# The last eight rows of a diffusion layer: second halves finished one row later and stored from GpSimd, and the inverse root from two sums on GpSimd

## The chip, the cores and the metric

The program runs on one core of one Trainium2 chip. The time is device time of one execution in microseconds (us); three runs of the kernel before gave a median of 1449.69 us (1447.68 to 1451.36).

## The reference, cut to what matters

One layer over 1024 tokens of 1024 values: normalisation, a combined projection into retention and differential attention, an output projection with a gated residual, then normalisation, a gated MLP with a depthwise convolution and a second gated residual. The change touches only the last two lines, the residual of the MLP and the final RMSNorm:

```
x = x + g1 * y_lat
h2 = rms_norm(x, norm2_g[l]) * (1.0 + sc2) + sh2
x = x + g2 * conv_ffn(h2, w_up[l], conv_w[l], conv_b[l], w_down[l])
...
return rms_norm(x, final_g)
def rms_norm(x, g):
    xf = x.astype(jnp.float32)
    y = xf * lax.rsqrt(jnp.mean(xf * xf, axis=-1, keepdims=True) + EPS)
    return (y * g.astype(jnp.float32)).astype(x.dtype)
```

## The kernel before, in words

The kernel computes float32 products from three passes on TensorE (`passes`, L127): each operand is split into a high and a low part, and high by high, high by low and low by high are added up in PSUM. ScalarE makes the high part (L908, L1227), VectorE the low part (L909, L1228).

The last stage (from L1211 on) is the down projection of the MLP, by a scheme of block sums and differences that needs seven block products in place of eight. The 1024 tokens are eight **rows** (tiles of 128 tokens), the 1024 output columns two **halves** of 512. `acc[t]` in SBUF is row t, 128 partitions by 1024. PSUM banks `c1` and `c2` hold four rows of one half each. When the products that fill the other three quarters of the output are done, they are copied or added into `acc` (L1265, L1270). What is left is the first half of rows 4 to 7, in `c1[0]` to `c1[3]`: eleven pairs of block operands, of which the first seven run over all four rows at once (L1333), each followed by `rows_before(m)` for m below 4, and the last four run row by row (L1337), so that `c1[0]` is complete first and `c1[3]` last.

A row is finished in these steps, and the names are used below:

- **load**: the row's residual `x1t` comes from DRAM on SyncE's DMA queue (L1274), into one of four buffers;
- **product** (L1276), VectorE: times the gate `g2bc`; for rows 4 to 7 the first half is read from PSUM;
- **sum** (L1277), VectorE: plus the residual;
- **square** (L1279), ScalarE: squares half a row and adds them up into one value per token, `sm4[:, t, c]`;
- **two small operations** on VectorE, 128x1 each: the two half sums are added (L1282), then divided by 1024 and EPS is added (L115, in `rsqrt`);
- **power**, GpSimd (L116): to the power of minus one half;
- **scale**, VectorE (L1287): times the power and times `fg`, the final gain. Rows 0 to 3 are scaled whole (128x1024) and stored from SyncE's queue (L1288). Rows 4 to 7 have had their second half multiplied by `fg` early (L1328, the **gain product**), so at the end ScalarE scales that half (L1343, the **second-half scale**) and VectorE the first (L1287), with one store each, both from SyncE's queue (L1344, L1288).

`rows_before(m)` does the second half of row m, finishes row m, and does the second half of row 4 + m. The code is written in this order, but a scheduler in the framework sets the final order of instructions on each engine from estimates of its own, and each engine then works through its own list strictly in that order; waits are on semaphores. An instruction that waits holds up all that stands behind it on its engine.

Of the kernel before, what the change touches and what calls it, by code (L numbers as in the profile page):

```python
# [11 lines left out]
AF = mybir.ActivationFunctionType  # L12
ALU = mybir.AluOpType
# [4 lines left out]
P = 128  # L18
D = 1024
# [10 lines left out]
EPS = 1e-6  # L30
# [43 lines left out]
def kernel(  # L74
# [16 lines left out]
    nc = tc.nc  # L91
# [17 lines left out]
    mhalf = kp.tile([P, 32], F32, name="mhalf")  # L109
# [4 lines left out]
    def rsqrt(out_ap, in_ap, mul, eps, n):  # L114
        nc.vector.tensor_scalar(out=out_ap, in0=in_ap, scalar1=mul, scalar2=eps, op0=ALU.mult, op1=ALU.add)  # L115
        nc.gpsimd.tensor_tensor(out=out_ap, in0=out_ap, in1=mhalf[:, :n], op=ALU.pow)  # L116
# [36 lines left out]
    with ExitStack() as p1:  # L153
# [495 lines left out]
        with tc.tile_pool(name="rc0", bufs=1) as r0:  # L649
# [20 lines left out]
            acc = r0.tile([P, 8], F32, name="acc")  # L670
# [58 lines left out]
        class Unit:  # L729
# [57 lines left out]
            def rstd(self):  # L787
                nc.vector.scalar_tensor_tensor(out=self.ss, in0=self.e, scalar=EPS * P, in1=self.ss, op0=ALU.mult, op1=ALU.add)
                self.pool_ins = nc.gpsimd.tensor_tensor(out=self.ss, in0=self.ss, in1=mhalf[:, :1], op=ALU.pow)
# [248 lines left out]
    def bank(name, pool=None):  # L1038
        return (next(bank_cycle) if pool is None else pool).tile([P, 512], F32, name=name, tag="bank")
# [49 lines left out]
    with ExitStack() as p4:  # L1089
# [93 lines left out]
        C = 512  # L1183
# [8 lines left out]
        def step(pd, a, b, first, last, more=False, ts=range(4)):  # L1192
            for t in ts:
                passes(pd[t], tuple(g[:, t * P : (t + 1) * P] for g in a), b, first, last, more)

        c1 = [bank(f"c1_{t}", psB if t < 2 else psC) for t in range(4)]
# [14 lines left out]
    with ExitStack() as p5:  # L1211
# [6 lines left out]
        def a_pair(i, m, n=2, alone=False):  # L1218

            raw = raw_load(next(slots), a_d[i][m].rearrange("p c (a b) -> p (c a) b", b=P)) if n == 2 else wst.tile([P, KD, P], F32, name=next(slots))  # L1220
            if n == 1:
                nc.sync.dma_start(out=raw[:, 0:4, :], in_=a_d[i][m][:, 0, :].rearrange("p (a b) -> p a b", b=P))
            raw = flat(raw)[:, : n * C]
            if alone:
                return [split1(raw[:, c * C : (c + 1) * C]) for c in range(n)]
            o = dop.tile([P, 2, 2 * C], F32R, name="ghl")
            nc.scalar.copy(o[:, 0, : n * C], raw)  # L1227
            nc.vector.tensor_tensor(out=o[:, 1, : n * C], in0=raw, in1=r32(o[:, 0, : n * C]), op=ALU.subtract)  # L1228
            return [tuple(o[:, a, c * C : (c + 1) * C] for a in range(2)) for c in range(n)]
# [25 lines left out]
        acc = [fin.tile([P, D], F32, name=f"acc{t}") for t in range(NT)]  # L1255
        g2bc = fin.tile([P, D], F32, name="g2bc")
        nc.sync.dma_start(out=g2bc, in_=g2_d)
        fg = fin.tile([P, D], F32, name="fg")
        nc.sync.dma_start(out=fg, in_=rows[0, R_FG : R_FG + D].partition_broadcast(P))
        sm4 = fin.tile([P, NT, 2], F32, name="sm4")  # L1260
        halves = [slice(0, C), slice(C, D)]

# [9 lines left out]
        def residual(t, c, src=None):  # L1272
            xt = fin.tile([P, C], F32, name="x1t", bufs=4)
            nc.sync.dma_start(out=xt, in_=x1_d[t][:, halves[c]])  # L1274
            dst = acc[t][:, halves[c]]
            nc.vector.tensor_tensor(out=dst, in0=dst if src is None else src, in1=g2bc[:, halves[c]], op=ALU.mult)  # L1276
            nc.vector.tensor_tensor(out=dst, in0=dst, in1=xt, op=ALU.add)  # L1277
            jk = fin.tile([P, C], BF16, name="jk", bufs=2)
            nc.scalar.activation(jk, dst, AF.Square, accum_out=sm4[:, t, c : c + 1])  # L1279

        def rstd(t):
            nc.vector.tensor_tensor(out=sm4[:, t, 0:1], in0=sm4[:, t, 0:1], in1=sm4[:, t, 1:2], op=ALU.add)  # L1282
            rsqrt(sm4[:, t, 0:1], sm4[:, t, 0:1], 1.0 / D, EPS, 1)

        def scaled(t, c0, c1_):
            x_ = acc[t][:, c0:c1_]
            nc.vector.scalar_tensor_tensor(out=x_, in0=x_, scalar=sm4[:, t, 0:1], in1=fg[:, c0:c1_], op0=ALU.mult, op1=ALU.mult)  # L1287
            nc.sync.dma_start(out=out[t * P : (t + 1) * P, c0:c1_], in_=x_)  # L1288
# [5 lines left out]
        for m in range(M):  # L1294
            s2, s1 = a_pair(1, m)
            t1 = split1(W[m, 0, 0])
            less(W[m, 0, 0], W[m, 1, 1], W[m, 0, 0])
            step(c1, s2, split1(W[m, 0, 0]), False, m == M - 1, True)
            step(c2, s1, t1, m == 0, m == M - 1)
            less(W[m, 1, 0], W[m, 1, 0], W[m, 0, 0])  # L1300
            if m < 4:
                first_difference(M - 4 + m)
            if 2 <= m < 6:
                residual(m - 2, 0)
# [16 lines left out]
        def rows_before(m):  # L1321
            if m < 4:
                residual(m, 1)
                rstd(m)
                scaled(m, 0, D)
                residual(4 + m, 1)
                dst = acc[4 + m][:, C:]
                nc.vector.tensor_tensor(out=dst, in0=dst, in1=fg[:, C:], op=ALU.mult)  # L1328
# [4 lines left out]
        for m in range(M - 4):  # L1333
            step(c1, a22s[m], T4s[m], False, False, True)
            rows_before(m)
        late_ops = list(zip(a22s, T4s))[M - 4 :]
        for t in range(4):  # L1337
            for i, ops in enumerate(late_ops):
                step(c1, *ops, False, i == 3, True, [t])
            r = 4 + t  # L1340
            residual(r, 0, c1[t])
            rstd(r)
            nc.scalar.activation(acc[r][:, C:], acc[r][:, C:], AF.Copy, scale=sm4[:, r, 0:1])  # L1343
            nc.sync.dma_start(out=out[r * P : (r + 1) * P, C:], in_=acc[r][:, C:])  # L1344
            scaled(r, 0, C)


def shape_constants():
# [75 lines left out]
```

## Time and profile before

| What | Value |
| --- | --- |
| Median of 3 runs | 1449.69 us (1447.68 to 1451.36) |
| Span of the profiled execution, first to last instruction | 1444.3 us |
| Between the span and the median | 5.4 us |
| Mean granted TensorE clock | 0.992 |
| TensorE busy | 1391.0 us (96%) |
| VectorE busy | 1013.2 us (70%) |
| ScalarE busy | 738.7 us (51%) |
| GpSimd busy | 336.4 us (23%) |

The profile gives the span of the profiled execution, from its first instruction to its last; what a timed run has beside that is not in the trace. Busy time of one engine overlaps that of the others. A timeline row gives the start and the duration in us, then engine, line, operation, output and inputs, shapes and count; in square brackets at its end stands how long the engine was idle before it and what released it. PE is TensorE, DVE VectorE, ACT ScalarE, POOL GpSimd, SPq the DMA queue of SyncE.

### The profile page before, as it was taken

The numbers are of one execution on the slowest core, as the hardware profiler recorded it, in microseconds if no ns is written. First come the engines' busy times: TensorE is split into PE (matmuls) and PEld (weight loads), VectorE is DVE, ScalarE is ACT, GpSimd is POOL, SyncE is SP. The second block draws the span as 40 slices with busy tenths as digits, with TensorE's granted clock in tenths as the row PEclk, the third lists the DMA queues.
The fourth block names the chain that finished last, engine by engine and source line by source line (L and its number), as shares of the span: only waits on it lengthen the run. The fifth ranks groups of instructions, "written<-read, shape, count | busy, mean of one in ns | idle before, by whom it ended". The sixth has DMA issues, their size and how long they took to land.

```text
span 1444.3 us, 19462 instructions
## 1 busy us (share of the span) xinstructions
PE 1391.0 (96%) x6924; PEld 1143.5 (79%) x6924; DVE 1013.2 (70%) x1509; ACT 738.7 (51%) x1409; POOL 336.4 (23%) x450
## 2 busy tenths in 40 slices
PE   7999999999899989999999999999999999999996
PEld 2587888788778779999888877888888888888885
DVE  4687454443677588889455988788777777998457
ACT  4565212232355688998414654555555545455533
POOL 0220000022688422431121043222223320000001
PEclk9999999999999999999999999999999999999999
DMA  7548754466456676680422122222222224952224
GB/s 283 218 144 292 241 190 161 161 190 189 129 160 194 161 180 157 149 150 2 187 77 85 73 89 110 110 109 99 86 90 106 109 109 166 391 208 103 102 95 175
DMA packets 107529, 217.77 MB, mean 151 GB/s; under 512 B 8932, under 2 KB 47332, under 8 KB 106536
## 3 DMA queue, kind: packets, MB, share of 16 engines
q1 hardware_dynamic: 99304, 191.62, 38.2%
q0 software_dynamic: 8128, 24.91, 7.8%
q8 instruction: 55, 0.90, 0.3%
q14 instruction: 42, 0.34, 0.1%
HBM read 159.08 MB, written 57.41 MB: 150 GB/s over the span
## 4 chain that ended last, share of the span: by engine, by line
PE 69%; DVE 8%; issue 6%; DMA 6%; POOL 3%; ACT 3%; SPq 0%; POOLq 0%; DVEq 0%; ACTq 0%
PE pv L774 5%; PE pA L742 5%; PE chain L130 5%; PE chain L132 5%; PE chain L131 5%; PE c L132 4%; PE c L131 4%; PE c L130 4%; PE pn L132 3%; PE pn L130 3%; PE pn L131 3%; PE third L132 2%; PE third L130 2%; PE third L131 2%; PE pt L762 2%
## 5 line engine op out<-in xcount | busy, mean ns | idle before, releaser
L130 PE MATMUL chain<-T,whi 128*128 128x512 f32 x264 | 103.7, 393 | 5.8 <-ACT ub L1152 3.1
L130 PE MATMUL pl<-hT,whi 128*128 128x512 f32 x256 | 107.6, 422 | 0.7 <-ACT hT L583 0.7
L131 PE MATMUL chain<-T,whi 128*128 128x512 f32 x264 | 103.5, 392 | 0.0
L132 PE MATMUL chain<-T,wlo 128*128 128x512 f32 x264 | 103.1, 391 | 0.0
L131 PE MATMUL pl<-hT,whi 128*128 128x512 f32 x256 | 101.6, 397 | 1.6 <-DVE sm L115 1.3
L132 PE MATMUL pl<-hT,wlo 128*128 128x512 f32 x256 | 100.9, 394 | 0.0
L745 DVE TENSOR_REDUCE mt<-pA 128x1 f32<-128x1280 f32 x64 | 95.3, 1490 | 3.3 <-PE pA L742 1.2
L742 PE MATMUL pA<-ks,qhl 128*128 128x512 f32 (+1 forms) x384 | 91.4, 374 | 5.0 <-ACT p L749 5.0
L132 PE MATMUL c<-whi,ghl 128*128 128x512 f32 x232 | 90.4, 390 | 0.2 <-DVE ghl L1228 0.2
L130 PE MATMUL c<-whi,ghl 128*128 128x512 f32 x232 | 90.3, 389 | 0.0
L131 PE MATMUL c<-wlo,ghl 128*128 128x512 f32 x232 | 90.2, 389 | 0.0
L749 ACT ACTIVATE p<-pA,mt 128x1280 f32<-128x1280 f32 x64 | 85.5, 1336 | 4.6 <-DVE mt L745 4.5
L116 POOL TENSOR_TENSOR sm<-sm,mhalf 128x1 f32<-128x1 f32 x26 | 16.7, 641 | 294.9 <-DVE sm L115 294.8
L1057 POOL TENSOR_TENSOR cmb<-wrb 128x512 f32<-128x512 f32 x20 | 26.8, 1341 | 250.1 <-DMA wrb<-w_up 135.9
L908 ACT CAST whi<-cmb 128x512 fp32r<-128x512 f32 x62 | 38.6, 623 | 87.1 <-PE chain L131 65.3
L742 PEld LDWEIGHTS pA<-ks,qhl 128*128 128x128 f32 x384 | 68.8, 192 | 17.6 <-ACT p L749 6.1
L130 PE MATMUL pn<-whi,hT 128*128 128x512 f32 x192 | 77.8, 405 | 0.0
L774 PE MATMUL pv<-va,aT 128*128 128x128 f32 x640 | 77.0, 275 | 0.1
L399 ACT ACTIVATE st<-pn 128x512 f32<-128x512 f32 x30 | 17.9, 598 | 114.7 <-PE pn L132 97.2
L908 ACT CAST whi<-wra 128x512 fp32r<-128x512 f32 x55 | 33.7, 622 | 82.9 <-PE third L131 42.3
L132 PE MATMUL pn<-whi,hT 128*128 128x512 f32 x192 | 75.5, 393 | 0.0
L131 PE MATMUL pn<-wlo,hT 128*128 128x512 f32 x192 | 75.1, 391 | 0.0
(320 smaller groups left out, 4006.2 us busy)
## 6 DMA issues: line engine op xcount, KB each, us to landing
wm<-w_mod SPq DMA_DIRECT2D x32, 512.0 KB, 4.4
raw<-w_in SPq DMA_DIRECT2D x28, 512.0 KB, 4.5
wra<-w_up SPq DMA_DIRECT2D x24, 512.0 KB, 3.2
wrb<-w_up SPq DMA_DIRECT2D x23, 512.0 KB, 3.5
W<-w_down SPq DMA_DIRECT2D x44, 256.0 KB, 6.0
ad<-s SPq DMA_DIRECT2D x20, 512.0 KB, 3.7
wra<-ad SPq DMA_DIRECT2D x20, 512.0 KB, 3.2
wrb<-ad SPq DMA_DIRECT2D x18, 512.0 KB, 4.1
```

The source lines that it names most:

```text
L116: nc.gpsimd.tensor_tensor(out=out_ap, in0=out_ap, in1=mhalf[:, :n], op=ALU.pow)
L130: mm(ps, lh, rh, start=first, stop=False, skip_group_check=more)
L131: mm(ps, lh, rl, start=False, stop=False, skip_group_check=more)
L132: mm(ps, ll, rh, start=False, stop=last, skip_group_check=more)
L399: nc.scalar.activation(st.rearrange("p h e -> p (h e)"), pt, func, scale=scale)
L742: mm(self.pa[m][:, c0:c1], self.q[:, i, m, qs], self.k[:, m, c0:c1], start=(i == 0), stop=(i == 1))
L745: nc.vector.tensor_reduce(out=self.mt[:, m : m + 1], in_=self.pa[m][:, :LK], axis=AX.X, op=ALU.min)
L749: nc.scalar.activation(self.p[m], self.pa[m][:, :LK], AF.Exp, scale=-1.0, bias=self.mt[:, m : m + 1], accum_out=self.s[:, m : m + 1])
L762: nc.tensor.transpose(self.pt[g][:, i, :], self.p[0][:, (4 * g + i) * P : (4 * g + i + 1) * P], ident)
L774: mm(self.pv, self.aT[:, c, :], self.v[:, c, :], start=(c == 0), stop=(c == NKT - 1))
L908: nc.scalar.copy(hi, src)
L1057: nc.gpsimd.tensor_tensor(out=s1, in0=b1, in1=b2, op=ALU.add)
```

## The change

Four edits, all in the last stage:

1. `fg` is multiplied by the square root of 1024 once, on GpSimd, right after it is loaded. With that the division of the sum by 1024 is no longer needed.
2. After the square of a second half, GpSimd adds 1024 times EPS to that half's sum (128x1).
3. `rstd` no longer uses VectorE: GpSimd adds the two sums (128x1) and takes the power.
4. For rows 4 to 7 the finishing steps (second-half scale, both stores, scale) move into `finished(r)`, which is called after the next row's product, sum, square and power; the store of the second half is issued from GpSimd's queue in place of SyncE's.

```
         fg = fin.tile([P, D], F32, name="fg")
         nc.sync.dma_start(out=fg, in_=rows[0, R_FG : R_FG + D].partition_broadcast(P))
+        nc.gpsimd.tensor_scalar(out=fg, in0=fg, scalar1=float(D) ** 0.5, scalar2=None, op0=ALU.mult)
...
             nc.scalar.activation(jk, dst, AF.Square, accum_out=sm4[:, t, c : c + 1])
+            if c:
+                nc.gpsimd.tensor_scalar(out=sm4[:, t, 1:2], in0=sm4[:, t, 1:2], scalar1=D * EPS, scalar2=None, op0=ALU.add)
 
         def rstd(t):
-            nc.vector.tensor_tensor(out=sm4[:, t, 0:1], in0=sm4[:, t, 0:1], in1=sm4[:, t, 1:2], op=ALU.add)
-            rsqrt(sm4[:, t, 0:1], sm4[:, t, 0:1], 1.0 / D, EPS, 1)
+            s0, s1 = sm4[:, t, 0:1], sm4[:, t, 1:2]
+            nc.gpsimd.tensor_tensor(out=s0, in0=s0, in1=s1, op=ALU.add)
+            nc.gpsimd.tensor_tensor(out=s0, in0=s0, in1=mhalf[:, :1], op=ALU.pow)
...
+        def finished(r):
+            nc.scalar.activation(acc[r][:, C:], acc[r][:, C:], AF.Copy, scale=sm4[:, r, 0:1])
+            nc.gpsimd.dma_start(out=out[r * P : (r + 1) * P, C:], in_=acc[r][:, C:])
+            scaled(r, 0, C)
+
         for t in range(4):
             for i, ops in enumerate(late_ops):
                 step(c1, *ops, False, i == 3, True, [t])
-            r = 4 + t
-            residual(r, 0, c1[t])
-            rstd(r)
-            nc.scalar.activation(acc[r][:, C:], acc[r][:, C:], AF.Copy, scale=sm4[:, r, 0:1])
-            nc.sync.dma_start(out=out[r * P : (r + 1) * P, C:], in_=acc[r][:, C:])
-            scaled(r, 0, C)
+            residual(4 + t, 0, c1[t])
+            rstd(4 + t)
+            if t:
+                finished(3 + t)
+        finished(7)
```

In the changed program the lines of the steps move: product L1277, sum L1278, square L1280, EPS added L1282, the two sums added L1286, power L1287, scale L1291, its store L1292, gain product L1332; the second-half scale stays at L1343 and its store is L1344. Below, acc_11675 to acc_11682 are rows 0 to 7, c_0 to c_3 the PSUM banks of rows 4 to 7, and sm_11687 (sm_11688 in the changed program) is `sm4`.

First place: VectorE around the scale of row 1 (acc_11676). Before:

```order
L1277 TENSOR_TENSOR acc_11676<-acc_11676,x1t 128x512
L1276 TENSOR_TENSOR acc_11680<-acc_11680,g2bc 128x512
L1276 TENSOR_TENSOR acc_11677<-acc_11677,g2bc 128x512
L1282 TENSOR_TENSOR sm_11687<-sm_11687 128x1
L1277 TENSOR_TENSOR acc_11680<-acc_11680,x1t 128x512
L115 TENSOR_SCALAR sm_11687<-sm_11687 128x1
L1277 TENSOR_TENSOR acc_11677<-acc_11677,x1t 128x512
L1287 SCALAR_TENSOR_TENSOR acc_11676<-acc_11676,sm_11687,fg 128x1024
```

The same place in the changed program:

```order
L1278 TENSOR_TENSOR acc_11676<-acc_11676,x1t 128x512
L1278 TENSOR_TENSOR acc_11680<-acc_11680,x1t 128x512
L1277 TENSOR_TENSOR acc_11677<-acc_11677,g2bc 128x512
L1291 SCALAR_TENSOR_TENSOR acc_11676<-acc_11676,sm_11688,fg 128x1024
L1332 TENSOR_TENSOR acc_11680<-acc_11680,fg 128x512
```

Between the sum of row 1 and its scale stood four large operations and the two small ones; now two large ones stand there.

Second place: VectorE at the end, from the product of row 6 (acc_11681) on. Before:

```order
L1276 TENSOR_TENSOR acc_11681<-c_2_11108,g2bc 128x512
L1287 SCALAR_TENSOR_TENSOR acc_11679<-acc_11679,sm_11687,fg 128x512
L1282 TENSOR_TENSOR sm_11687<-sm_11687 128x1
L1277 TENSOR_TENSOR acc_11681<-acc_11681,x1t 128x512
L115 TENSOR_SCALAR sm_11687<-sm_11687 128x1
L1287 SCALAR_TENSOR_TENSOR acc_11680<-acc_11680,sm_11687,fg 128x512
L1282 TENSOR_TENSOR sm_11687<-sm_11687 128x1
L1276 TENSOR_TENSOR acc_11682<-c_3_11109,g2bc 128x512
L115 TENSOR_SCALAR sm_11687<-sm_11687 128x1
L1277 TENSOR_TENSOR acc_11682<-acc_11682,x1t 128x512
L1287 SCALAR_TENSOR_TENSOR acc_11681<-acc_11681,sm_11687,fg 128x512
```

In the changed program, from the gain product of row 7 on:

```order
L1332 TENSOR_TENSOR acc_11682<-acc_11682,fg 128x512
L1277 TENSOR_TENSOR acc_11680<-c_1_11107,g2bc 128x512
L1291 SCALAR_TENSOR_TENSOR acc_11679<-acc_11679,sm_11688,fg 128x512
L1278 TENSOR_TENSOR acc_11680<-acc_11680,x1t 128x512
L1277 TENSOR_TENSOR acc_11681<-c_2_11108,g2bc 128x512
L1278 TENSOR_TENSOR acc_11681<-acc_11681,x1t 128x512
L1291 SCALAR_TENSOR_TENSOR acc_11680<-acc_11680,sm_11688,fg 128x512
L1291 SCALAR_TENSOR_TENSOR acc_11681<-acc_11681,sm_11688,fg 128x512
L1277 TENSOR_TENSOR acc_11682<-c_3_11109,g2bc 128x512
L1278 TENSOR_TENSOR acc_11682<-acc_11682,x1t 128x512
L1291 SCALAR_TENSOR_TENSOR acc_11682<-acc_11682,sm_11688,fg 128x512
```

The scale of row 6 (acc_11681), which stood behind the product and the sum of row 7 (acc_11682), now stands ahead of both. The scale of row 4 (acc_11679) stood behind the product of row 6; it now stands ahead of the sum of row 5 and the product of row 6.

Third place: GpSimd's list at its end. Before, from its last stores of block operands on:

```order
L1108 DMA ad_10_113<-tconv 128x512 x2
L1114 DMA ad_5_141<-tconv 128x512
L1118 DMA ad_10_124<-s_11216 128x1024
L1120 DMA ad_10_135<-s_11018 128x1024
L116 TENSOR_TENSOR sm_11687<-sm_11687,mhalf 128x1 x8
```

In the changed program, from the two sums of row 4 on:

```order
L1286 TENSOR_TENSOR sm_11688<-sm_11688 128x1
L1287 TENSOR_TENSOR sm_11688<-sm_11688,mhalf 128x1
L1344 DMA out_dram<-acc_11679 128x512
L1286 TENSOR_TENSOR sm_11688<-sm_11688 128x1
L1287 TENSOR_TENSOR sm_11688<-sm_11688,mhalf 128x1
L1344 DMA out_dram<-acc_11680 128x512
L1286 TENSOR_TENSOR sm_11688<-sm_11688 128x1
L1287 TENSOR_TENSOR sm_11688<-sm_11688,mhalf 128x1
L1344 DMA out_dram<-acc_11681 128x512
L1286 TENSOR_TENSOR sm_11688<-sm_11688 128x1
L1287 TENSOR_TENSOR sm_11688<-sm_11688,mhalf 128x1
L1344 DMA out_dram<-acc_11682 128x512
```

Where eight powers stood, each row now has its additions, its power and, for rows 4 to 7, a store that stands ahead of the next row's addition. On ScalarE the second-half scale of each of the rows 4 to 6 now stands ahead of the next row's square; before, the squares of rows 5 and 6 stood ahead of the second-half scales of rows 4 and 5, and the scale of row 6 already ahead of the square of row 7.

## The prediction

> **What bounds the kernel now.** I read the page first, then busy time by stretch, then VectorE's timeline from 1408 us on.
>
> ```profile
> span 1444.3 us, 19462 instructions
> ```
> ```profile
> core 0: us, PE busy (x) PEld busy (x) DVE busy (x) ACT busy (x) POOL busy (x), PEclk, DMA share, GB/s
> ...
> 1257.00:1408.00 151.00, 151.00 (x668) 125.02 (x667) 107.56 (x147) 73.14 (x112) 0.00 (x0) 1.00 0.39 139
> 1408.00:1433.20 25.20, 25.20 (x112) 20.53 (x110) 23.65 (x45) 9.26 (x23) 3.82 (x5) 1.00 0.48 167
> 1433.20:1444.30 11.10, 0.01 (x1) 0.00 (x0) 4.68 (x12) 3.41 (x7) 2.09 (x3) 0.70 0.51 189
> ```
>
> TensorE is busy without a gap until 1433.2 us, and nothing in the change feeds it but what hides in the stretch to 1408. So the change can only move the 11.1 us behind TensorE. VectorE is nearly full before that point (23.65 of 25.20 us): it carries a backlog into the end, and its order decides. These are its rows there (and the scales of rows 0 to 3 ahead of them):
>
> ```profile
> 1413.47 1.28 DVE L1287 SCALAR_TENSOR_TENSOR acc<-acc,sm,fg 128x1024 f32<-128x1024 f32 x1 [0.46 <-POOL sm L116]
> ...
> 1418.94 1.28 DVE L1287 SCALAR_TENSOR_TENSOR acc<-acc,sm,fg 128x1024 f32<-128x1024 f32 x1 [0.44 <-POOL sm L116]
> ...
> 1422.60 1.28 DVE L1287 SCALAR_TENSOR_TENSOR acc<-acc,sm,fg 128x1024 f32<-128x1024 f32 x1 [0.44 <-POOL sm L116]
> ...
> 1427.70 1.28 DVE L1287 SCALAR_TENSOR_TENSOR acc<-acc,sm,fg 128x1024 f32<-128x1024 f32 x1
> ...
> 1430.82 0.69 DVE L1277 TENSOR_TENSOR acc<-acc,x1t 128x512 f32<-128x512 f32 x1
> 1431.43 0.15 DVE L1282 TENSOR_TENSOR sm<-sm 128x1 f32<-128x1 f32 x1
> ...
> 1431.69 0.68 DVE L1276 TENSOR_TENSOR acc<-c,g2bc 128x512 f32<-128x512 f32 x1
> 1432.43 0.75 DVE L1287 SCALAR_TENSOR_TENSOR acc<-acc,sm,fg 128x512 f32<-128x512 f32 x1
> 1433.10 0.15 DVE L1282 TENSOR_TENSOR sm<-sm 128x1 f32<-128x1 f32 x1
> 1433.17 0.69 DVE L1277 TENSOR_TENSOR acc<-acc,x1t 128x512 f32<-128x512 f32 x1
> 1433.78 0.15 DVE L115 TENSOR_SCALAR sm<-sm 128x1 f32<-128x1 f32 x1
> ...
> 1435.33 0.68 DVE L1276 TENSOR_TENSOR acc<-c,g2bc 128x512 f32<-128x512 f32 x1
> ...
> 1436.04 0.69 DVE L1277 TENSOR_TENSOR acc<-acc,x1t 128x512 f32<-128x512 f32 x1
> ...
> 1439.55 0.75 DVE L1287 SCALAR_TENSOR_TENSOR acc<-acc,sm,fg 128x512 f32<-128x512 f32 x1 [0.66 <-POOL sm L116]
> ```
> ```profile
> 1440.30 0.33 SPq L1344 DMA_DIRECT2D out_dram<-acc  x1
> 1440.72 0.38 SPq L1288 DMA_DIRECT2D out_dram<-acc  x1
> ```
> ```profile
> L1288 SPq DMA_DIRECT2D out_dram<-acc x8: 332/338/382, 1414.8 to 1440.7; - x8
> ...
> DMA to landing us min/median/max: 2.3/2.3/2.3
> ```
>
> Start to start, a large operation of 512 takes 0.60 (1430.82 to 1431.43), a scale of 512 0.67 (1432.43 to 1433.10), a dependent product 0.71 (1435.33 to 1436.04), a small operation 0.07 (1433.10 to 1433.17). The last row's scale starts at 1439.55, the last of its two stores is issued at 1440.72 and lands 2.3 later, at 1443.02; 1.28 of closing work follows to 1444.3. Waits ahead of the scales of rows 0 to 3 sum to 1.34, and row 4 waits nowhere.
>
> **The change: rows 0 to 4.** Removed from VectorE up to row 4's scale: ten small operations, 0.70. Their work goes to GpSimd, onto the path between a row's sum and its scale. Its prices:
>
> ```profile
> 1434.00 0.55 POOL L116 TENSOR_TENSOR sm<-sm,mhalf 128x1 f32<-128x1 f32 x1 [1.60 <-DVE sm L115]
> 1436.15 0.99 POOL L116 TENSOR_TENSOR sm<-sm,mhalf 128x1 f32<-128x1 f32 x1 [1.59 <-DVE sm L115]
> ```
> ```profile
> L785 POOL TENSOR_TENSOR e<-sa x32: 184/189/214, 511.4 to 694.3; 128x1 f32<-128x1 f32 x32
> ```
> ```profile
> L232 POOL TENSOR_SCALAR ks<-kvgf,kd 128x128 f32<-128x128 f32 x64 | 29.7, 465 | 98.2 <-PE pub L335 59.1 <-DMA kvgc<-kvg 32.9 <-issue 1.9
> ```
> ```profile
> 1433.95 0.63 ACT L1279 ACTIVATE jk<-acc 128x512 bf16<-128x512 f32 x1 [0.79 <-DVE sm L115]
> 1434.49 0.19 ACT L1279 ACTIVATION_READ_ACCUMULATOR jk<-acc 128x1 f32 x1
> 1434.59 0.72 ACT L1343 ACTIVATE acc<-acc,sm 128x512 f32<-128x512 f32 x1
> ```
>
> No row shows a 128x1 addition on GpSimd at this place; I take 0.19 (L785, same shape and engine). The ends are 0.15, as VectorE's, and 0.46, the mean of the 128x128 operation. A power takes 0.55, but 0.99 where VectorE's sum of 1436.04 runs beside it: GpSimd is held until that ends.
>
> From the end of a row's sum, then: 0.09 to ScalarE (1433.86 to 1433.95), square and read-out 0.73, 0.07 to GpSimd (1433.93 to 1434.00 is that step behind VectorE's L115), EPS 0.19, a step 0.08, addition 0.19, a step 0.08, power 0.55, 0.04 to VectorE (1434.55 to 1434.59): 2.02 us. For rows 4 to 7 the EPS was added long before, and it is 1.75. Behind rows 1, 2 and 3 the new order leaves two large operations between sum and scale, 1.20, of which 0.08 overlaps the sum's own end: 1.12. Each of these rows waits 0.90. Row 4 has the gain product and one product, 1.22: 0.53. Row 0 has 1.66 of splitting work, and its square starts 0.23 late behind ScalarE's splits: 0.59. That is 3.8 in all. GpSimd is also held by VectorE's large operations beside it: I take 0.2 in each of four rows (half of 0.99 less 0.55; the ends are none, and 0.44 in each), so 4.6, where 1.34 stood.
>
> In the old order row 5's sum (0.61) and row 6's product (0.74) stood ahead of row 4's scale; now they are behind it, 1.35 less. Row 4's scale: 1432.43 + 4.6 - 1.34 - 0.70 - 1.35 = 1433.6.
>
> **Rows 5 to 7.** Row 5: row 4's scale 0.67, its own sum 0.69, then 1.75 with GpSimd held 0.35 by row 6's sum: 1437.1. The scale of row 6 stands next, and its square waits behind row 5's second-half scale: that 0.63, square 0.72, then 0.94 (of 1.75 what lies behind the square). In front of row 6's addition GpSimd also has to issue row 5's store. How long that takes, and how late it starts, is seen at another store:
>
> ```profile
> 1235.14 0.68 DVE L1117 TENSOR_TENSOR s<-s,tconv 128x512 f32<-128x512 f32 x1
> ...
> 1236.12 0.54 POOL L1118 DMA_DIRECT2D ad<-s  x1 [1.32 <-DVE s L1117]
> ```
>
> It starts 0.30 behind its releaser (1235.82 to 1236.12) and takes 0.54 to 0.6: done 1.6 after row 5's scale, some 0.15 later than the square. So row 6's scale starts 2.45 after row 5's, at 1439.5. Queued behind that wait are the product and the sum of row 7, although `c1[3]` is ready from 1433.2 on. Row 7: 0.67 + 0.71 + 0.69 + 1.75 = 3.8, so its scale starts at 1443.3 where it was 1439.55: **3.75 later**. Loads and stores on SyncE's queue stay ahead of their users: a load's buffer comes free several large operations before its row needs it.
>
> **The last store.** It leaves GpSimd behind ScalarE's 0.72 and the 0.30. Landing of 256 KB from GpSimd's queue:
>
> ```profile
> L856 POOL DMA_DIRECT2D woraw<-w_out x8: 567/590/608, 519.2 to 610.2; - x8
> ...
> DMA to landing us min/median/max: 3.0/3.2/8.2
> ```
> ```profile
> L1108 POOL DMA_DIRECT2D ad<-tconv x1: 622/622/622, 1216.2 to 1216.2; - x1
> ...
> DMA to landing us min/median/max: 3.4/3.4/3.4
> ```
>
> I take 3.2: 0.72 + 0.30 + 3.2 = 4.22 from scale to landing, where it was 3.47 (1439.55 to 1443.02): **0.75 later**. The ends are 2.3 (SyncE's) and 3.4. The 8.2 belongs to a crowded queue; here two stores share it. The Trainium skill ("DMA: Bandwidth & Descriptors", section "Anatomy of one DMA — SWDGE (gpsimd) path") gives 2.0 us plus bytes over 436e3 for such a transfer, 2.6 here: no row is that short, and by it the sum would be 0.6 less, just inside 0.3%.
>
> **`fg` on GpSimd.** It follows this load at once, and GpSimd has nothing else to do from there to 1408.
>
> ```profile
> 1262.55 0.33 SPq L1259 DMA_DIRECT2D fg<-rows  x1
> ```
> ```profile
> L349 POOL TENSOR_SCALAR kvgc<-kvgc,kd 128x256 f32<-128x256 f32 x4 | 2.5, 620 | 0.0
> ```
>
> From 128 to 256 values a one-scalar operation grows from 0.465 to 0.620, so 1024 values take about 0.465 + 7 x 0.155 = 1.55. It can hold VectorE once; TensorE is fed without a gap in that stretch and VectorE is idle for 43 of its 151 us. With that cover I take nothing; without it up to 1.55 would reach the end.
>
> **Sum.** 3.75 + 0.75 = 4.5 us on the span of 1444.3, 1448.8. The profiled span stands 5.4 below the median; the difference is laid on the median: 1454.2.
>
> **The rivals.** A median of this kernel can tell about 0.3%, 4.35 us, from no change: the forecast lies at that edge.
>
> - *GpSimd's additions are dear.* At 0.46 each: twelve of them on the path (two for rows 0 to 3, one for rows 4 to 7), 3.2 more: 1457.4. For it: it is GpSimd's nearest one-scalar row. Against: that row is 128 values wide.
> - *GpSimd is hardly held, and its store lands like SyncE's.* 4.5 - 1.15 - 0.9 = 2.45: 1452.1. Against it is the 0.99. The Trainium skill ("Trainium Kernel Development and Optimization", section "Key Constraints") says that issuing from several engines only saves the sequencer's issue time; the saving would be 0.42 here (1440.30 to 1440.72) in place of my 0.75, so 3.3 in all, 1453.0. The rows of 3.0 to 3.4 speak against it.
> - *GpSimd's chain is covered, and it ends no slower.* If the scales of rows 0 to 4 didn't wait, row 4's would start at 1429.0; then TensorE leads, whose row 6 is complete twelve products of 0.225 (25.20 us for 112) before row 7, at 1430.5. Row 6: product and sum to 1431.9, square behind row 5's second-half scale to 1432.7, scale at 1433.7, row 7's at 1437.5, landing 1441.7: 1.3 faster, 1448.4. It would decide from where GpSimd's operations and steps, 1.20 of the 2.02, take 0.3; the power alone is 0.55.
> - *The change doesn't do what it says.* Row 6 is to finish behind row 7's sum. If it did, row 7's square would follow row 6's second-half scale at once (1439.5 + 0.63 + 0.72 + 0.94 = 1441.8 for row 7's scale), worth 1.5. But the list of VectorE has row 6's scale ahead of row 7's product, and is fixed; that is in the forecast and has no chance of its own.
>
> **How the numbers follow.** Forecast 0.56, of which 0.33 above the edge (held powers, 3.4 for the store and `fg` push up); dear additions 0.23; cheap GpSimd 0.16; covered chain 0.04; something faster that I don't see 0.01. Slower by over 0.3%: 0.33 + 0.23 = 0.56; within: 0.23 + 0.16 + 0.04 = 0.43; faster: 0.01. Low end: cheapest additions (0.5 less), none held (1.15), store at 2.3 (0.9) leave 1.95, 1451.6. High end: the dear case and half of what holding can add in rows 1 to 5 (0.24 each), 1458.0.
>
> **What would show it.** TensorE's last product still ends at 1433.2. The scales of rows 1 to 3 wait 0.9 to 1.2 on GpSimd; row 4's starts at 1433.6, row 6's waits over 1.5 on GpSimd, row 7's product starts near 1440.2. GpSimd's 128x1 additions take 0.19 alone, its last store lands 3.0 to 3.4 after issue, behind SyncE's. I am wrong if VectorE reaches row 7's product by 1436, or if the additions take 0.4.

## The result, and the profile after

The changed kernel takes 1452.8 us (median of ten runs, 1450.31 to 1459.94), the kernel before 1449.53 in the ten runs beside them (1447.38 to 1451.36). The ratio is 1.0033, with a 95% interval of 1.0018 to 1.0048: it is slower, by about what can be told from no change.

The profiled execution of the changed kernel is its slowest: 1459.94 us, span 1458.2. Its TensorE finished 8 us later than in the profiled execution before (1441.23 against 1433.21). Nothing shows the change as the cause of that: over all the kernels profiled below, this end lies anywhere from 1431.8 to 1441.2, for the one that has VectorE's and ScalarE's lists of the changed kernel (e7_eps_early) it is 1438.15, and for one with the instructions of before up to its last power 1436.24. What repeats is what lies behind: each kernel was profiled once, but in the three pairs below that share VectorE's list of the last rows and what feeds it, the last scale stands at the same distance from the last product to 0.01 us (6.34 and 6.35, 9.94 twice, 5.15 twice). So the two are compared by the **tail**, from the end of TensorE's last product to the end of the span: 11.10 us before, 16.95 after. Busy time by stretch, of the changed kernel (the first is where `fg` is multiplied, the second the 25.2 us ahead of the last product's end, the third the tail):

```profile
core 0: us, PE busy (x) PEld busy (x) DVE busy (x) ACT busy (x) POOL busy (x), PEclk, DMA share, GB/s
1270.00:1290.00 20.00, 20.00 (x90) 16.57 (x89) 18.26 (x25) 11.02 (x17) 3.35 (x1) 1.00 0.70 264
1416.03:1441.23 25.20, 25.19 (x112) 20.52 (x110) 20.94 (x30) 7.78 (x20) 6.72 (x18) 1.00 0.50 165
1441.23:1458.17 16.94, 0.00 (x0) 0.00 (x0) 6.20 (x9) 4.95 (x10) 5.41 (x11) 0.61 0.34 128
```

In the second stretch VectorE is busy for 20.94 where it was 23.65, and the small operations that went (ten of 0.15) are only part of that: it waits. Its timeline says for whom (the first and the last scale of rows 0 to 3, then all from row 4's on), and what GpSimd and SyncE do at the end:

```profile
1420.75 1.28 DVE L1291 SCALAR_TENSOR_TENSOR acc<-acc,sm,fg 128x1024 f32<-128x1024 f32 x1 [1.05 <-POOL sm L1287]
...
1436.72 1.28 DVE L1291 SCALAR_TENSOR_TENSOR acc<-acc,sm,fg 128x1024 f32<-128x1024 f32 x1 [1.03 <-POOL sm L1287]
...
1440.84 0.39 PE L132 MATMUL c<-W,wlo 128*128 128x512 f32 x1
...
1441.71 0.75 DVE L1291 SCALAR_TENSOR_TENSOR acc<-acc,sm,fg 128x512 f32<-128x512 f32 x1 [0.57 <-POOL sm L1287]
...
1443.97 0.48 POOL L1286 TENSOR_TENSOR sm<-sm 128x1 f32<-128x1 f32 x1 [0.58 <-ACT jk L1280]
...
1445.12 0.75 DVE L1291 SCALAR_TENSOR_TENSOR acc<-acc,sm,fg 128x512 f32<-128x512 f32 x1 [0.73 <-POOL sm L1287]
...
1446.14 0.58 POOL L1344 DMA_DIRECT2D out_dram<-acc  x1 [1.05 <-ACT acc L1343]
...
1446.74 0.21 POOL L1286 TENSOR_TENSOR sm<-sm 128x1 f32<-128x1 f32 x1
...
1447.62 0.75 DVE L1291 SCALAR_TENSOR_TENSOR acc<-acc,sm,fg 128x512 f32<-128x512 f32 x1 [1.75 <-POOL sm L1287]
1448.29 0.68 DVE L1277 TENSOR_TENSOR acc<-c,g2bc 128x512 f32<-128x512 f32 x1
...
1449.01 0.69 DVE L1278 TENSOR_TENSOR acc<-acc,x1t 128x512 f32<-128x512 f32 x1
...
1451.47 0.75 DVE L1291 SCALAR_TENSOR_TENSOR acc<-acc,sm,fg 128x512 f32<-128x512 f32 x1 [1.76 <-POOL sm L1287]
1452.25 0.33 SPq L1292 DMA_DIRECT2D out_dram<-acc  x1
1452.49 0.58 POOL L1344 DMA_DIRECT2D out_dram<-acc  x1 [1.05 <-ACT acc L1343]
```

The last scale stands 10.24 us behind the last product (1441.23 to 1451.47); before it was 6.34 (1433.21 to 1439.55). That is 3.9 of the 5.85 us. Row 7's product starts only at 1448.29, though its bank is full from 1441.23 on: row 6's scale stands ahead of it and waits 1.75 us for GpSimd.

The other 1.95 lie behind the last scale: from its start to the end of the span it is now 6.70 us, and was 4.76. The last store, from GpSimd's queue, explains only part of that. This view of its line gives the issues, and the time from issue to landing:

```profile
L1344 POOL DMA_DIRECT2D out_dram<-acc x4: 584/584/664, 1442.7 to 1452.5; - x4
...
DMA to landing us min/median/max: 2.6/2.6/2.7
```

So it lands at 1452.49 + 2.63 = 1455.12, but the span ends at 1458.17. The closing instructions of the program (all on one line, L1429) show who is late (name, count, shortest, median and longest duration in ns, first and last start in us):

```profile
L1429 SPq EVENT_SEMAPHORE  x11: 17/28/2326, 1452.6 to 1458.1; - x11
...
L1429 POOLq DRAIN  x3: 46/102/4927, 1452.5 to 1457.9; - x3
L1429 SPq DRAIN  x3: 7/7/7, 1455.5 to 1457.7; - x3
```

And the same view of the kernel before:

```profile
L1420 POOLq DRAIN  x3: 46/93/4596, 1438.9 to 1444.0; - x3
L1420 SPq DRAIN  x3: 7/7/7, 1443.4 to 1443.8; - x3
```

SyncE has seen every landing at 1455.5 and drains in 7 ns. GpSimd's first DRAIN lasts 4.93 us: it starts at 1452.46, beside GpSimd's last instruction (the issue of the store, done at 1453.07), and ends at 1457.39. The engines then meet, and 0.78 later the program is over. Before, GpSimd's DRAIN ended at 1443.53, 4.01 behind the end of the last power, and SyncE was done at 1443.43: both count from row 7's power, and the two ends lay only 0.09 apart (0.08 to 0.09 in four runs below that place that power and the stores in the same way), so the wait for GpSimd was easy to miss.

### The profile page after: what moved, and what is told of

It is laid out like the page before. It is cut to its first block, busy times and chain, and to the rows that moved or that the text cites. A ratio compares the mean times of both kernels' runs of the same rounds, so it can differ in the third digit from the quotient of the medians.

```text
span 1458.2 us, 19469 instructions
## 1 busy us (share of the span) xinstructions
PE 1396.7 (96%) x6924; PEld 1146.5 (79%) x6924; DVE 1012.8 (69%) x1493; ACT 740.2 (51%) x1409; POOL 344.4 (24%) x471
## 4 chain that ended last, share of the span: by engine, by line
PE 68%; DVE 7%; DMA 7%; issue 6%; POOL 3%; ACT 3%; SPq 0%; POOLq 0%; DVEq 0%; ACTq 0%
PE pv L774 5%; PE chain L130 5%; PE pA L742 5%; PE chain L131 5%; PE chain L132 5%; PE c L132 4%; PE c L130 3%; PE c L131 3%; PE pn L131 3%; PE pn L132 3%; PE pn L130 3%; PE pt L762 2%; PE third L131 2%; PE third L130 2%; PE third L132 2%
## 5 line engine op out<-in xcount | busy, mean ns | idle before, releaser
L774 PEld LDWEIGHTS pv<-va,aT 128*128 128x128 f32 x640 | 74.0, 192 | 0.7 <-DVE yT L803 0.3
```

What stands on the lines that cost most here:

```text
L774: mm(self.pv, self.aT[:, c, :], self.v[:, c, :], start=(c == 0), stop=(c == NKT - 1))
```

## The experiments

Two theories on the closing. **A**: the end follows GpSimd's last instruction by some 4.0 to 4.3 us, whatever it is, and a store on GpSimd's queue puts that instruction later. **B**: GpSimd's store itself is slow, and the end follows its landing. On the rest my theory was the prediction's: VectorE waits for GpSimd's chain, and the order of VectorE's list puts row 7 behind such a wait.

All tails in one table; times are us behind the end of the last product (the span of the fourth column is on the trace's own scale). Each row is one execution; SyncE is done when its first closing DRAIN starts.

| Run | Last scale starts | Tail | Span | GpSimd's DRAIN ends | SyncE is done | Last scale to end |
| --- | --- | --- | --- | --- | --- | --- |
| before | 6.34 | 11.10 | 1444.31 | 10.32 | 10.23 | 4.76 |
| after | 10.24 | 16.95 | 1458.17 | 16.16 | 14.26 | 6.70 |
| e1_sp_store | 9.94 | 14.70 | 1449.58 | 13.92 | 13.83 | 4.76 |
| e2_gp_tail | 6.35 | 14.71 | 1450.96 | 13.92 | 10.25 | 8.36 |
| e3_power_alone | 9.94 | 14.71 | 1449.01 | 13.92 | 13.83 | 4.77 |
| e4_order_alone | 5.63 | 10.39 | 1447.43 | 9.61 | 9.53 | 4.76 |
| e5_forced | 6.37 | 13.15 | 1445.62 | 12.36 | 10.55 | 6.78 |
| e6_forced_sp | 5.15 | 9.92 | 1446.30 | 9.13 | 9.05 | 4.77 |
| e7_eps_early | 9.01 | 15.71 | 1453.86 | 14.93 | 13.03 | 6.70 |
| e8_scalar_store | 5.15 | 9.97 | 1442.37 | 9.13 | 9.13 | 4.82 |
| e9_sqrt | 5.87 | 11.01 | 1446.49 | 1.61 | 10.17 | 5.13 |
| e10_all_behind | 4.51 | 10.97 | 1442.81 | 8.48 | 10.14 | 6.46 |
| e11_two_behind | 5.04 | 10.24 | 1445.82 | 9.02 | 9.41 | 5.20 |

**The stores alone.**

```
 def finished(r):
     nc.scalar.activation(acc[r][:, C:], acc[r][:, C:], AF.Copy, scale=sm4[:, r, 0:1])
-    nc.gpsimd.dma_start(out=out[r * P : (r + 1) * P, C:], in_=acc[r][:, C:])
+    nc.sync.dma_start(out=out[r * P : (r + 1) * P, C:], in_=acc[r][:, C:])
```

> The changed kernel with the second halves of rows 4 to 7 stored from SyncE's queue again; everything else as changed. Measured by the tail, from the end of TensorE's last product to the end of the span: 11.1 us before, 16.95 after. Theory A (the end of the program follows GpSimd's last instruction by some 4.0 to 4.3 us, and 0.8 more): GpSimd's last instruction is now the last power, so scale to end falls from 6.70 to about 4.75, and rows 5 and 6 no longer have a store issue ahead of their additions (0.1): tail 14.9, time some 2.0 us below the changed kernel, 1450.8. Theory B (GpSimd's store itself is slow to land and the end follows its landing): scale to end 4.76 as well, the same 14.9. My prediction's own terms (0.75 for the store): 16.2. Last scale stays 10.1 to 10.2 behind the last product in all of them.

The tail is 14.70. Time 1451.34 against 1446.98 for the kernel before on the same chip (1.0029, 1.0015 to 1.0043). The last rows, and the longest closing DRAIN, of this run's timeline and closing line:

```profile
1444.24 0.55 POOL L1287 TENSOR_TENSOR sm<-sm,mhalf 128x1 f32<-128x1 f32 x1
1444.82 0.72 ACT L1343 ACTIVATE acc<-acc,sm 128x512 f32<-128x512 f32 x1 [0.93 <-POOL sm L1287]
1444.83 0.75 DVE L1291 SCALAR_TENSOR_TENSOR acc<-acc,sm,fg 128x512 f32<-128x512 f32 x1 [1.75 <-POOL sm L1287]
```
```profile
L1429 POOLq DRAIN  x3: 46/93/4594, 1444.2 to 1449.3; - x3
```

The stores cost the changed kernel 2.25 us of its 5.85: 0.30 ahead of the last scale (0.23 of it in row 6, whose addition no longer stands behind a store issue), and 1.94 behind it. Both theories expect that; the prediction's own terms, with a tail of 16.2, don't fit.

**GpSimd busy longer, without a store.** In the kernel before, twelve additions of 128x1 more, behind row 7's last step; nothing waits for them.

```
+    last, power = sm4[:, 7, 1:2], sm4[:, 7, 0:1]
+    nc.gpsimd.tensor_tensor(out=last, in0=power, in1=power, op=ALU.add)
+    for _ in range(11):
+        nc.gpsimd.tensor_tensor(out=last, in0=last, in1=power, op=ALU.add)
```

> The kernel before, with twelve further 128x1 additions on GpSimd, one after the other, behind row 7's power; no store and no other engine waits for them. They end about 12 x 0.27 = 3.2 us behind the last power. Theory A (the end follows GpSimd's last instruction by 4.0 and 0.8): the tail grows from 11.1 to about 14.3, although every store has landed long before. Theory B (the end follows the landing of the last store): tail unchanged, 11.1.

The tail is 14.71; the last scale stays (6.35), and SyncE is done at 10.25, as before.

```profile
1442.91 3.25 POOL L1349 TENSOR_TENSOR sm<-sm 128x1 f32<-128x1 f32 x11
1443.34 0.33 SPq L1344 DMA_DIRECT2D out_dram<-acc  x1
1443.77 0.39 SPq L1288 DMA_DIRECT2D out_dram<-acc  x1
```
```profile
L1424 POOLq DRAIN  x3: 46/102/4241, 1445.9 to 1450.7; - x3
L1424 SPq DRAIN  x3: 7/7/7, 1446.5 to 1450.4; - x3
```

The additions end at 1446.15, GpSimd's DRAIN 4.01 later at 1450.16; SyncE was done at 1446.5. Theory A holds, B falls: additions that nobody waits for make the tail 3.6 us longer, with no store on GpSimd's queue at all.

**The written order alone.** Edit 4 in the kernel before, with all stores from SyncE and the sums on VectorE.

```
-            r = 4 + t
-            residual(r, 0, c1[t])
-            rstd(r)
-            nc.scalar.activation(acc[r][:, C:], acc[r][:, C:], AF.Copy, scale=sm4[:, r, 0:1])
-            nc.sync.dma_start(out=out[r * P : (r + 1) * P, C:], in_=acc[r][:, C:])
-            scaled(r, 0, C)
+            residual(4 + t, 0, c1[t])
+            rstd(4 + t)
+            if t:
+                finished(3 + t)
+        finished(7)
```

> Edit 4 without the rest: finishing steps one row later in the code, but the sums, the division and EPS on VectorE as before, fg as it was, all stores from SyncE's queue. VectorE's list now has row 6's scale behind row 7's product and sum, and ScalarE squares row 6 behind row 5's second-half scale. If the order in the code was the harm, the tail grows; by my step rules (square of row 6 done 1.45 later than before, one small operation between row 7's product and sum waits 0.1 for it, row 7's sum at 1436.15, last scale at 1439.05 against 1439.55) the tail is 10.6, 0.5 shorter than before: time 1449.0.

The tail is 10.39, 0.7 shorter than before; the time is the same (1447.49 against 1446.98; 1.0000, 0.9988 to 1.0013). Its VectorE from row 7's product on:

```profile
1438.79 0.69 DVE L1276 TENSOR_TENSOR acc<-c,g2bc 128x512 f32<-128x512 f32 x1
...
1439.57 0.69 DVE L1277 TENSOR_TENSOR acc<-acc,x1t 128x512 f32<-128x512 f32 x1
...
1440.99 0.75 DVE L1287 SCALAR_TENSOR_TENSOR acc<-acc,sm,fg 128x512 f32<-128x512 f32 x1 [0.66 <-POOL sm L116]
...
1442.67 0.75 DVE L1287 SCALAR_TENSOR_TENSOR acc<-acc,sm,fg 128x512 f32<-128x512 f32 x1 [0.66 <-POOL sm L116]
```

Here row 6's scale (1440.99) does stand behind row 7's product and sum, and it helps a little. So the idea of edit 4 isn't the harm.

**The root from GpSimd alone.** Edits 1 to 3, with the last rows finished in their own turn (the diff above, reversed, in the changed kernel).

> Edits 1 to 3 alone: the root from GpSimd, but the last rows finished in their own turn in the code, as before, and stored from SyncE. The instruction lists of all five engines are the same as in the run that only took the stores back to SyncE, so the tail must be that run's: 14.7. If it is, calling the finishing steps one row later in the code adds nothing here.

The tail is 14.71, with each scale where the run with SyncE's stores has it. Together: edits 1 to 3 cost 14.70 - 11.10 = 3.60 us, the stores on GpSimd 2.25, and the written order nothing, because with the sums gone from VectorE the scheduler arrives at one and the same list whichever way the code is written.

**The written order enforced.** The changed kernel, VectorE and ScalarE held to the code's order by dependencies without a wait.

```
+        start = len(nc.cur_bb.bb.instructions)
         for t in range(4):
...
         finished(7)
+        in_order(start, FORCE[1:3])
```

> The changed kernel with one difference: VectorE and ScalarE are held to the order in which the last four rows are written, so that each scale stands behind the next row's product and sum. GpSimd keeps the whole chain and the stores. My prediction gave row 6's place alone 1.5 us. By the step rules the whole order is worth more: row 4's scale stays near 0.5 behind the last product, then six large operations without a wait to row 7's sum (its end 4.6 behind), last scale 6.4 (10.25 in the changed kernel): 3.85 less. Closing by theory A (GpSimd's last instruction, a store issue, plus 4.3 and 0.8): 6.7, tail 13.1. By theory B, with the end 1.28 behind the landing: tail 11.4.

Last scale 6.37, tail 13.15. The last rows of its VectorE (row 7's sum, row 6's scale, row 7's scale):

```profile
1436.38 0.69 DVE L1278 TENSOR_TENSOR acc<-acc,x1t 128x512 f32<-128x512 f32 x1
1436.99 0.74 DVE L1291 SCALAR_TENSOR_TENSOR acc<-acc,sm,fg 128x512 f32<-128x512 f32 x1
1438.84 0.75 DVE L1291 SCALAR_TENSOR_TENSOR acc<-acc,sm,fg 128x512 f32<-128x512 f32 x1 [1.10 <-POOL sm L1287]
```

Only one wait is left behind row 4. The order is worth 3.87 us of the last scale, which with it is where it was before the change (6.34). GpSimd's chain in rows 0 to 3 still costs: row 4's scale starts 0.54 behind the last product, where before it was 0.77 ahead. From there on the chain is covered by other work but for the last wait, and that makes the loss good. And the closing, 6.78, fits theory A again: the last store is issued until 7.92, lands at 10.19, and the end is 13.15.

**EPS off the path.** The changed kernel, EPS added to the half that is ready first.

```
-            if c:
-                nc.gpsimd.tensor_scalar(out=sm4[:, t, 1:2], in0=sm4[:, t, 1:2], scalar1=D * EPS, scalar2=None, op0=ALU.add)
+            if c == (t >= 4):
+                nc.gpsimd.tensor_scalar(out=sm4[:, t, c : c + 1], in0=sm4[:, t, c : c + 1], scalar1=D * EPS, scalar2=None, op0=ALU.add)
```

> The changed kernel with one difference: GpSimd adds EPS to the half of a row that is ready first, so that this step (0.19 and 0.08) is off the path in rows 0 to 3; VectorE's and ScalarE's lists are those of the changed kernel. If GpSimd's chain is on the path in each of these rows, as the waits of 1.03 to 1.05 ahead of their scales say, row 4's scale comes 4 x 0.27 = 1.1 earlier (at 0.6 ahead of the last product's end instead of 0.49 behind), and the last scale and the tail follow: tail 15.9. If VectorE's backlog covers the chain, nothing moves: 16.95. If GpSimd's steps here cost 0.36 to 0.72 because they are held, up to 2 less.

Tail 15.71. Row 4's scale and the last, where TensorE ends at 1438.15:

```profile
1437.42 0.75 DVE L1291 SCALAR_TENSOR_TENSOR acc<-acc,sm,fg 128x512 f32<-128x512 f32 x1 [0.57 <-POOL sm L1287]
...
1447.16 0.75 DVE L1291 SCALAR_TENSOR_TENSOR acc<-acc,sm,fg 128x512 f32<-128x512 f32 x1 [1.76 <-POOL sm L1287]
```

Row 4's scale is 0.73 ahead of the last product's end where it was 0.49 behind: 1.22 earlier, 0.31 for each of rows 0 to 3, and all of it reaches the end (1.24). GpSimd's chain is on the path in each of the rows 0 to 3.

**All three together**: the order, EPS early, stores from SyncE.

> The changed kernel with three differences: VectorE and ScalarE are held to the order in which the last four rows are written (row r's scale behind row r+1's product and sum), EPS goes to whichever half of a row is ready first (so that it is off the path in rows 0 to 3), and all stores go from SyncE's queue. By the step rules: four EPS steps of 0.27 off the path put row 4's scale 0.6 ahead of the last product's end (after: 0.48 behind it); then six operations to row 7's sum, which ends 3.46 behind; row 7's scale 1.75 later, at 5.2 (before 6.3, after 10.2); closing 4.76: tail 10.0, 1.1 below the kernel before, time 1448.4. If the order is not the cause of the late last scale, it stays near 9.

```profile
1441.53 0.75 DVE L1291 SCALAR_TENSOR_TENSOR acc<-acc,sm,fg 128x512 f32<-128x512 f32 x1 [1.08 <-POOL sm L1287]
```

TensorE's last product ends at 1436.38 here: last scale 5.15, tail 9.92, the shortest of all; time 1446.7 against 1446.98 (0.9996, 0.9981 to 1.0010). It is 7.0 us of tail ahead of the changed kernel, and 1.2 ahead of the kernel before, the last of which a measurement of the whole can't tell from nothing.

**Who binds then?** As before, GpSimd and SyncE end together (9.13 and 9.05). To part them, row 7's second half went out from ScalarE's queue:

```
+    store = nc.scalar if r == 7 else nc.sync
-    nc.sync.dma_start(out=out[r * P : (r + 1) * P, C:], in_=acc[r][:, C:])
+    store.dma_start(out=out[r * P : (r + 1) * P, C:], in_=acc[r][:, C:])
```

> The run with VectorE and ScalarE in written order, EPS early and SyncE's stores (tail 9.92), with one difference: row 7's second half is stored from ScalarE's queue, so that SyncE issues row 7's other store 0.42 earlier. There GpSimd's closing work ended 9.13 behind the last product and SyncE's 9.06. Theory A: GpSimd's end still decides, tail 9.85. Theory B: the last landing decides, tail 9.5.

```profile
1438.30 0.40 ACTq L1345 DMA_DIRECT2D out_dram<-acc  x1
1438.33 0.33 SPq L1292 DMA_DIRECT2D out_dram<-acc  x1
```

Tail 9.97, and it doesn't part them (both end at 9.13): the two stores were issued at once, 0.4 earlier than the later one was, yet the last landing stayed at 8.6 behind the last product (8.62, and 8.60 from SyncE alone). The Trainium skill ("Trainium Kernel Development and Optimization", section "Key Constraints") says that issuing from several engines saves only the issue time; the trace agrees that nothing more is saved, and here not even that came out at the end.

**The root off GpSimd.** For rows 4 to 7 ScalarE takes the square root and VectorE the reciprocal.

```
+            if t >= 4:
+                nc.scalar.activation(sm4[:, t, 0:1], sm4[:, t, 0:1], AF.Sqrt, bias=sm4[:, t, 1:2])
+                return
...
         def finished(r):
+            nc.vector.reciprocal(sm4[:, r, 0:1], sm4[:, r, 0:1])
```

> As the run before it, and for rows 4 to 7 the root leaves GpSimd: ScalarE takes the square root of the two sums right behind the square, VectorE the reciprocal ahead of the scale (128x1 each). GpSimd's last instruction is then an EPS addition long before the end. No run shows ScalarE's root here; by its read-out of 128x1 (0.19) and VectorE's small operations (0.07 to 0.15) the step from square to scale falls from 0.94 to about 0.55, less what ScalarE's loading of another function table costs row 4 (unknown, once). Last scale 5.0 behind the last product; closing 0.75, 0.38 and 2.3 less the 0.33 of the other store's issue, and 1.28: 4.35. Theory A: GpSimd no longer binds, tail 9.35, time about 1.7 us (0.12%) below the kernel before. Theory B: same tail. Only if the program's end has some other cause is it still 9.9.

Tail 11.01, last scale 5.87; 1448.11 against 1448.46 (0.9995, 0.9981 to 1.0008).

```profile
1433.89 1.28 ACT L1286 ACT_TABLE_LOAD   x1
...
1435.19 0.29 ACT L1286 ACTIVATE sm<-sm 128x1 f32<-128x1 f32 x1
...
1435.52 0.16 DVE L1346 RECIPROCAL sm<-sm 128x1 f32<-128x1 f32 x1 [0.59 <-ACT sm L1286]
...
1441.03 1.32 ACT L1347 ACTIVATE acc<-acc,sm 128x512 f32<-128x512 f32 x2
...
1442.38 0.37 ACTq L1349 DMA_DIRECT2D out_dram<-acc  x1
```
```profile
L1436 POOLq DRAIN  x3: 46/102/4557, 1432.5 to 1446.2; - x3
L1436 SPq DRAIN  x3: 7/7/7, 1445.7 to 1446.0; - x3
```

The tail of 9.35 that was expected was missed, and the gain went three ways: a table load of 1.28 us makes row 4's scale 0.9 later, each reciprocal costs VectorE 0.19 from start to start, and row 7's second-half scale stands behind row 6's on ScalarE (two in 1.32), so its store leaves at 1442.38. For the closing the run is the cleanest: GpSimd's last instruction is long past, its DRAIN ends 1.61 behind the last product, still 4.01 after that instruction, and now SyncE decides: it is done at 10.17, the end follows at 11.01.

**More scales behind row 7's sum.** As the shortest run, but all four scales, or three of them, behind row 7's product and sum.

```
             residual(4 + t, 0, c1[t])
             rstd(4 + t)
-            if t:
-                finished(3 + t)
-        finished(7)
+        for r in range(4, 8):
+            finished(r)
```

> As the run with VectorE and ScalarE in written order, EPS early and SyncE's stores (tail 9.92, last scale 5.15 behind the last product), but all four scales of rows 4 to 7 stand behind row 7's product and sum. By the step rules, if GpSimd isn't held: row 7's sum ends 2.15 behind the last product, its power 1.7 later, VectorE has three scales (2.0) to do until then: last scale 4.1, tail 8.9. If GpSimd is held by the three scales beside it (two inputs in SBUF, as beside the power of 0.99): its power can't start before row 6's scale ends at 4.1: last scale 4.7 to 4.9, tail 9.5 to 9.7. If the eight stores (2 MB behind 2.9) are too many for the queue, the landing of the last is later than 3.5 behind the last scale and scale to end exceeds 4.8.

> The same, but row 4's scale keeps its place ahead of row 6's product, and only the scales of rows 5 to 7 stand behind row 7's sum. By the step rules, not held: row 7's sum ends 2.8 behind the last product, chain 1.75: last scale 4.5, tail 9.3. Held by the scales of rows 5 and 6 (2.75 to 4.1): as above, 4.7 to 4.9, tail 9.5 to 9.7. Time some 1.6 us (0.1%) below the kernel before, within what can't be told from no change.

All four behind: last scale 4.51, tail 10.97 (1446.90 against 1447.29; 1.0000, 0.9983 to 1.0016). Three behind: 5.04 and 10.24 (1446.01 against 1447.29; 0.9990, 0.9975 to 1.0006). Both tails are longer than any that was expected (9.7 at most). The first one's GpSimd, VectorE and SyncE:

```profile
1433.84 2.07 DVE L1291 SCALAR_TENSOR_TENSOR acc<-acc,sm,fg 128x512 f32<-128x512 f32 x3
...
1434.05 0.94 POOL L1287 TENSOR_TENSOR sm<-sm,mhalf 128x1 f32<-128x1 f32 x1
...
1435.37 0.94 POOL L1287 TENSOR_TENSOR sm<-sm,mhalf 128x1 f32<-128x1 f32 x1
...
1436.35 0.75 DVE L1291 SCALAR_TENSOR_TENSOR acc<-acc,sm,fg 128x512 f32<-128x512 f32 x1 [0.44 <-POOL sm L1287]
...
1438.58 0.59 SPq L1292 DMA_DIRECT2D out_dram<-acc  x1
```

Two limits show. A power beside VectorE's scales takes 0.94 in place of 0.55, so three scales in a row slow down the very step that the fourth waits for; and the stores that pile up are issued late and slowly (the last at 1438.58, 1.48 us behind the end of the last scale, in 0.59), so from the last scale to the end it takes 6.46. GpSimd's DRAIN isn't the limit there: it ends at 8.48, SyncE is done at 10.14.

## Why the prediction was right and where it failed

The forecast of 1454.2 lies 1.4 above the measured 1452.8, inside the range, and the sign was right; but the sum under it, 4.5 us, is 1.35 less than the tail grew (5.85). That the forecast is this near is in part luck, as the point on the 5.4 us says. By its steps:

- *Only what lies behind TensorE's last product can move.* Right: 25.19 of 25.20 us busy up to it. That it would end at 1433.2 was wrong as a time, since this end differs by 9.4 us between the executions profiled.
- *Rows 0 to 4.* Right: the waits sum to 1.05 + 3 x 1.03 + 0.57 = 4.7 (4.6 predicted), row 4's scale stands 0.49 behind the last product (0.4 predicted). The sum fits better than its parts: row 0 waits 1.05, where 0.59 and a share of 0.2 for GpSimd being held were worked out. Inside it, additions cost 0.18 to 0.21 as taken, but the EPS step is dearer than the 0.27 taken: 0.31 each by its own experiment. The additions' dear price, the rival of 1457.4, was seen only once, at 1443.97 (0.48, beside row 6's sum), and the chain was not covered.
- *Rows 5 to 7.* Right: from scale to scale 3.41, 2.50 and 3.85 where 3.5, 2.45 and 3.8 were worked out; the last scale is 3.9 later, 3.75 predicted. GpSimd's store issue costs row 6 its share: 0.23 there, 0.30 in all, by the run without it.
- *The store.* Issue 0.30 behind ScalarE: right (1452.19 to 1452.49). Landing: 2.63, not the 3.2 taken from rows of GpSimd's queue earlier in the kernel, so it lands 3.65 after the scale, only 0.18 later than before (3.47), not 0.75. The Trainium skill ("DMA: Bandwidth & Descriptors", section "Anatomy of one DMA — SWDGE (gpsimd) path") gives 2.0 us plus bytes over 436e3, an estimate of 2.6 for 256 KB, and the trace agrees with it (2.62 to 2.67 for the four stores; in the run with the enforced order they took 2.37 to 2.81). Around the rows of 3.0 to 3.4 the DMA engines were busier (0.53 to 0.73 against 0.34 in the tail here), but no run shows that as the cause.
- *The closing is 1.28 behind the last landing.* **This step failed.** It is 1458.17 - 1455.12 = 3.05, 1.77 longer. The rule behind the 1.28 was wrong: the end waits for GpSimd's closing DRAIN too, 4.01 behind GpSimd's last computing instruction (4.32 behind the end of this store's issue), and the store on GpSimd's queue moved GpSimd's last instruction from 0.03 ahead of the last scale to 1.60 behind its start. From the last scale to the end the sum had 0.75 more, all of it for the landing; measured were 1.95, of which the landing is 0.18. The rival by which a second queue saves 0.42 fails at the same place. In the trace of before GpSimd's DRAIN already was the later of the two ends, by 0.09; I read SyncE's side alone.
- *`fg` on GpSimd is free.* Right, though the operation took 3.35 us where I took 1.55: TensorE worked through all of it (20.00 of 20.00 us in the first stretch above, GpSimd's 3.35 among them).
- *The 5.4 us laid on the median.* Of these only about 1.75 are there in each execution (1459.94 against the span of 1458.2); the rest was a short execution of before. That did no harm: to lay them on the span is to add 4.5 to the median of before, 1449.69, and beside the changed kernel it was 1449.53. The median grew by 3.3 (2.6 to 7.0 by its interval), less than the sum and less than the tail's 5.85, which lies in the interval. So a sum that was 1.35 too small met a median that grew by 2.6 less than the tail: that is the luck in the 1.4. No run shows why the median grew less; TensorE's end, which scatters by more than this, is a guess that wasn't tested.
- *The rival that the change doesn't do what it says* was right in its mechanism and priced too low: I gave row 6's place 1.5, but the order it asked for is worth 3.87, since rows 4, 5 and 6 all gain work between sum and scale. That the written order makes no difference to the list once the sums have left VectorE I hadn't seen.

## What to carry to other kernels

Read every engine's closing instructions before a last step is moved to another engine: the one whose end comes first today can be the one that the program waits for tomorrow, and two that end together hide each other. A chain on a slow engine is cheap as long as independent work stands between its start and its user in the user's list, and costs its full length where it doesn't; so look at the list that the scheduler makes, not at the order of the code. When executions differ by more than the change is worth, compare from an event that both share.

## What the runs showed of the hardware

GpSimd's closing DRAIN ends 4.01 us after its last computing instruction in ten of the thirteen kernels profiled, whether that was an addition, an EPS step or a power, and whether it came early or last; in the three others it ends 4.32, 4.32 and 4.44 behind the end of a store's issue. The program ends 0.78 to 0.84 us after the later of this DRAIN and SyncE's last wait. GpSimd's 128x1 operations stretch beside VectorE operations on two SBUF inputs (a power from 0.55 to 0.94, an addition from 0.19 to 0.48), and the one with 1024 values per partition took 2.81 to 3.35. Beside a product that VectorE reads from PSUM a power kept its 0.55 (at 1432.72 in the run with all four scales behind). ScalarE's square root cost 0.29 for 128x1 and 1.28 once for its table.

How far the stretching goes shows in the six runs with EPS early, about 150 us ahead of the end, where the first of the EPS additions for rows 0 to 3 falls into work of VectorE without a gap (here the run with the three changes together; the second view's columns are PE, PEld, DVE, ACT and POOL):

```profile
1294.06 21.14 POOL L1282 TENSOR_SCALAR sm<-sm 128x1 f32<-128x1 f32 x1 [17.39 <-ACT jk L1280]
```
```profile
1294.06:1315.20 21.14, 21.14 (x95) 17.48 (x94) 21.14 (x33) 13.18 (x23) 21.14 (x2) 1.00 0.45 143
```

This addition took 21.14 us beside 33 operations of VectorE without a gap; the last of the same four, where VectorE had paused for 0.10, took 0.20. Nothing waited for it there. The prices of GpSimd's chain at the end of the kernel, 0.18 to 0.72 a step, were measured where VectorE mostly waits for that chain, and can't be carried to a place where VectorE is full.
